# The q and k moves between partitions issued on GpSimd's DMA queue instead of SyncE's

## The chip, the cores and the metric

The kernel runs on one core of a Trainium2 chip. The metric is the device time of one launch in microseconds; shown is the median of three runs. A profiled execution of the same program gives the rows below; its own time stands beside its span.

## The reference

One transformer layer in float32 on 512 tokens and 16 meta tokens (T = 528), width 1024. `rmsnorm`, then one wide projection `u @ w_in` that yields the queries, keys and values of three kinds of attention and three gates; then a gated sum of the three, an output projection, and a gated convolutional feed-forward of width 2816.

```python
y_sb = _stick_breaking(q_sb, k_sb, v_sb)                 # 4 heads of 64
y_sp = _indexed_sparse_attention(norm(q_sp), norm(k_sp), v_sp, q_ix, k_ix, w_ix, ...)  # 4 heads, top 132 keys
y_df = _differential_attention(q1, q2, k1, k2, v_df, lam, ...)   # 4 heads, two score maps each
merged = (sigmoid(g_sb + b) * (y_sb @ w_br_sb) + sigmoid(g_sp + b) * (y_sp @ w_br_sp)
          + sigmoid(g_df + b) * (y_df @ w_br_df))
h = h + merged @ w_out
h = h + (silu(conv(gate)) * val) @ w_down                # gate, val = split(rmsnorm(h) @ w_up)
```

## The kernel before

Every float32 operand of a large product is held as two float32r parts, a high one and a rest (names ending in h and l), and a product is three passes on TensorE: high by high, rest by high, high by rest (`mm3`, L336). The third pass is the one that reads the rest of the weights, `wl`.

**Weights** come in 133 chunks of 128x1024 from `wpk`, in the order of a written plan (`PLAN`), and `prep(k)` (L315) readies them one chunk ahead of use. There are two ways. A chunk of the first kind is loaded raw by SyncE (`wr`, two buffers), cast to `wh` by ScalarE, and its rest `wl` is a subtraction on VectorE or GpSimd. Every second chunk from the eleventh to the output projection (the set `two`, L296) goes without a raw buffer: GpSimd issues a load into `wh` (`gdma`, L120), ScalarE writes minus that into `wl` (L332), and GpSimd issues a second load of the chunk that is added onto `wl` in flight (L334). In this text that is the accumulating load; there are 25. `wh` has three buffers and `wl` two, so ScalarE's write into `wl` waits until the third pass of the chunk two before it is done.

**Attention** runs in eight units: sb0, sb1, df0 to df3, sp0, sp1. For each, three dense products give raw queries, keys and values (`unit`, L1007), and between their matmuls small streams are ticked (L195) that do the rest. `q_stream` (L665) casts the queries to `a`, takes the rest `l`, and then issues three moves of 64 partitions each; `k_stream` (L683) does the same with four tiles and six moves. A move is a DMA from SBUF to SBUF which brings a head from partitions 64 to 127 to 0 to 63 or the other way, so that two heads' high and rest parts stand as one 128-row operand for `scores` (L761). In each group of three, the third move overwrites what the first two (in the keys' case) or the first (in the queries') read, and so waits until those have landed. In all 8 x 9 = 72 moves of 129 to 132 KB are issued, all by `move` (L659) on SyncE.

**Order.** The program is generated with a planner's clocks for the four engines (P TensorE, V VectorE, S ScalarE, G GpSimd). `book(e, cost)` (L77) advances one of them and the due time of the stream that is being ticked by the cost and 150 ns more. `sub` (L108) sends a subtraction to GpSimd or VectorE, whichever the clocks expect first. A unit's scores are not put into TensorE's order before the planner's clock passes the unit's due time: the time at the end of its moves plus 6500 (L681, L699) plus SLACK of 1800 (L882). A framework then sets each engine's order of instructions by its own forecast of when they become ready, and adds the semaphores. Each engine takes its instructions strictly in that order, and a DMA's waits are waited out by the engine that issues it.

**Queues.** SyncE issues the raw weights, the bias tables and, before the change, the moves. GpSimd issues the 25 + 25 loads of the second kind and the gathers of the bias tiles, and does a part of the subtractions and additions.

Of the kernel before, what the change touches and what calls it, by code (L numbers as in the profile page):

```python
# [8 lines left out]
F32 = mybir.dt.float32  # L9
# [46 lines left out]
def tile_kernel(ctx: ExitStack, tc, hT, wpk, par, bias, yT):  # L56
    nc = tc.nc
# [19 lines left out]
    def book(e, cost):  # L77
        c = cur[0]
        clock[e] = max(clock[e], clock["P"]) + cost
        c["t"] = max(clock[e], c["t"] + cost, clock["P"] + cost) + LAT  # L80
# [25 lines left out]
    G = Timed("G", nc.gpsimd, 2.3, 200)  # L106
# [550 lines left out]
        give("tmp", 4)  # L657

    def move(dst, src):  # L659
        nc.sync.dma_start(dst.bitcast(F32), src.bitcast(F32))  # L660

    def qtile():
        return ap_.tile([P, T], F32R, tag="qk", bufs=caps["qk"], name="qk")
# [1 line left out]
    def q_stream(unit, raw, gain):  # L665


        n = TQ
        if gain is not None:
            yield from headnorm(raw, n, gain, blk)  # L670
        yield from wait("qk", 2)
        yield from wait("tmp")
        a, b, l = qtile(), qtile(), tmp(F32R)
        S.copy(a[:, :n], raw[:, :n])
        sub(l[:, :n], raw[:, :n], a[:, :n])
        move(b[64:128, :n], a[64:128, :n])
        move(b[0:64, :n], l[64:128, :n])
        move(a[64:128, :n], l[0:64, :n])
        give("tmp", 2)
        unit["q"] = (a, b)  # L680
        unit["t"] = max(unit.get("t", 0), cur[0]["t"] + 6500)  # L681
# [594 lines left out]
```

## Time and profile before

| | us |
|---|---|
| three runs: median (lowest to highest) | 901.34 (894.71 to 905.32) |
| the profiled execution's own time | 900.03 |
| its span, first to last instruction | 898.2 |
| TensorE busy | 870.2 |
| VectorE busy | 536.1 |
| ScalarE busy | 454.6 |
| GpSimd busy | 248.9 |

The attention stage ends at about 470 us, the output projection at about 520, the feed-forward at 898. The moves run from 40.8 to 378.6 us. An engine's busy time does not hold its waits; idle time is given per releaser, which is inferred.

### The profile page before, as it was taken

The page shows a single profiled execution, that of the slowest core. Times are in us where ns is not written, and L with a number is a line of the kernel's source. Part 1 is how long each engine was busy: PE and PEld are TensorE (multiplying, and loading weights), DVE is VectorE, ACT ScalarE, POOL GpSimd, SP SyncE. Part 2 cuts the span into 40 slices and gives each one's busy share as a digit, 9 for nine tenths or more (in the row PEclk, how much of TensorE's full clock was granted, in tenths as well). Part 3 has the DMA queues.
Part 4 walks back from the last instruction along what each step waited for, and adds up shares of the span by engine and source line. Part 5 has one row for each costly group of instructions (what it writes and reads, how often), then busy time and mean ns, then how long its engine had stood idle before and what let it go on. Part 6 is the DMA issues. An engine that isn't in the chain of part 4 may idle for free.

```text
span 898.2 us, 15407 instructions
## 1 busy us (share of the span) xinstructions
PE 870.2 (97%) x6066; PEld 807.8 (90%) x6066; DVE 536.1 (60%) x1145; ACT 454.6 (51%) x848; POOL 248.9 (28%) x200
## 2 busy tenths in 40 slices
PE   7899999999999999799999999999999999999998
PEld 6888999999998999699999999999999999888886
DVE  7669969888887787686457544444454544322221
ACT  7457887787756687645553443333333333211110
POOL 2334012122112111664034234444444444200100
PEclk9999999999999999899999999999999999999999
DMA  6666635574547645544454323233333322333330
GB/s 235 163 177 210 163 86 124 133 168 111 121 109 156 164 105 137 120 125 92 121 118 164 96 94 94 94 94 94 95 93 95 92 88 92 103 117 106 118 104 27
DMA packets 35959, 107.79 MB, mean 120 GB/s; under 512 B 4713, under 2 KB 4857, under 8 KB 35888
## 3 DMA queue, kind: packets, MB, share of 16 engines
q1 hardware_dynamic: 27968, 78.19, 28.7%
q0 software_dynamic: 7920, 28.64, 14.9%
q8 instruction: 47, 0.77, 0.4%
q14 instruction: 24, 0.20, 0.1%
HBM read 93.99 MB, written 5.86 MB: 111 GB/s over the span
## 4 chain that ended last, share of the span: by engine, by line
PE 72%; DVE 9%; ACT 7%; DMA 6%; issue 5%; POOL 1%; SPq 1%; ACTq 0%; POOLq 0%; DVEq 0%
PE psd L183 50%; PE psw L183 21%; DVE tmp L99 4%; ACT tmp L99 3%; DMA wl<-wpk 2%; DMA qk<-qk 2%; PE psw L187 2%; DVE work L99 1%; DMA wr<-wpk 1%; DVE wl L99 1%; DMA wh<-wpk 1%; DVE m L99 1%; ACT wl L99 1%; ACT G L99 1%; ACT wh L99 1%
## 5 line engine op out<-in xcount | busy, mean ns | idle before, releaser
L99 ACT CAST wh<-wr 128x1024 fp32r<-128x1024 f32 (+2 forms) x112 | 114.1, 1021 | 201.6 <-DMA wr<-wpk 168.5
L99 DVE TENSOR_TENSOR wl<-wr,wh 128x1024 fp32r<-128x1024 f32 (+2 forms) x80 | 96.2, 1203 | 71.6 <-PE psd L183 67.9
L99 POOL TENSOR_TENSOR wl<-wr,wh 128x1024 fp32r<-128x1024 f32 x32 | 81.5, 2548 | 176.6 <-PE psd L183 95.0
L183 PE MATMUL psd<-xh,wh 128*128 128x258 f32 (+2 forms) x792 | 118.9, 289 | 4.0 <-DVE tmp L99 3.5
L183 PE MATMUL psd<-xl,wh 128*128 128x258 f32 (+2 forms) x792 | 118.2, 289 | 0.0
L183 PE MATMUL psd<-xh,wl 128*128 128x258 f32 (+2 forms) x792 | 116.7, 288 | 1.2 <-POOL wl L99 1.1
L183 PEld LDWEIGHTS psd<-xh,wh 128*128 128x128 f32 x792 | 104.7, 190 | 5.7 <-issue 3.6
L183 PEld LDWEIGHTS psd<-xh,wl 128*128 128x128 f32 x792 | 104.1, 190 | 2.4 <-POOL wl L99 1.3
L183 PEld LDWEIGHTS psd<-xl,wh 128*128 128x128 f32 x792 | 104.4, 191 | 0.5
L99 ACT ACTIVATE tmp<-tmp 128x528 f32<-128x528 f32 (+7 forms) x154 | 69.6, 475 | 17.2 <-DVE tmp L99 14.6
L99 POOL TENSOR_TENSOR ft<-ft 128x512 f32<-128x512 f32 x22 | 47.1, 2140 | 83.5 <-DVE ft L99 83.5
L99 DVE SCALAR_TENSOR_TENSOR ft<-ft,prm 128x512 f32<-128x512 f32 x44 | 48.0, 1090 | 30.1 <-ACT ft L99 29.3
L334 POOL DMA_DIRECT2D wl<-wpk x25 | 22.2, 888 | 130.1 <-ACT wl L99 105.6
L183 PE MATMUL psw<-uh,wh 128*128 128x256 f32 (+2 forms) x264 | 47.0, 320 | 0.0
L183 PE MATMUL psd<-ul,wh 128*128 128x258 f32 (+2 forms) x264 | 46.9, 319 | 0.0
L183 PE MATMUL psw<-ul,wh 128*128 128x256 f32 (+2 forms) x264 | 46.9, 319 | 0.0
L183 PE MATMUL psd<-uh,wl 128*128 128x258 f32 (+2 forms) x264 | 46.8, 319 | 0.0
L183 PE MATMUL psw<-uh,wl 128*128 128x256 f32 (+2 forms) x264 | 46.8, 319 | 0.0
L183 PE MATMUL psd<-uh,wh 128*128 128x258 f32 (+2 forms) x264 | 46.8, 319 | 0.0
L183 PE MATMUL psd<-al,wh 128*128 128x512 f32 x176 | 45.8, 396 | 0.0
L183 PE MATMUL psd<-ah,wl 128*128 128x512 f32 x176 | 45.8, 396 | 0.0
L183 PE MATMUL psd<-ah,wh 128*128 128x512 f32 x176 | 45.8, 396 | 0.0
(196 smaller groups left out, 1674.7 us busy)
## 6 DMA issues: line engine op xcount, KB each, us to landing
wr<-wpk SPq DMA_DIRECT2D x106, 512.0 KB, 3.6
wh<-wpk POOLq DMA_DIRECT2D x25, 512.0 KB, 3.9
wl<-wpk POOLq DMA_DIRECT2D x25, 512.0 KB, 5.6
qk<-qk SPq DMA_DIRECT2D x48, 132.0 KB, 2.5
gd<-tab SPq DMA_DIRECT2D x8, 328.0 KB, 5.5
tmp<-hT SPq DMA_DIRECT2D x8, 264.0 KB, 6.2
W<-gd POOLq DMA_DIRECT2D x8, 264.0 KB, 3.9
qk<-tmp SPq DMA_DIRECT2D x16, 128.5 KB, 4.4
```

The lines of the kernel that those rows point to most:

```text
L99: return f(out, *a, **k)
L183: PE.matmul(out, lhsT, rhs, **k)
L187: PE.transpose(out, x, ident[:x.shape[0], :x.shape[0]])
L334: nc.gpsimd.dma_start(wl, chunk(a), accum_op=OP.add)
```

## The change

`move` issues its DMA on GpSimd's queue, and books 650 ns on the planner's GpSimd clock, which also puts 650 + 150 ns on the stream's due time for each move. Nothing else is edited; sources, destinations and the dependences among the moves are as before.

```diff
     def move(dst, src):
-        nc.sync.dma_start(dst.bitcast(F32), src.bitcast(F32))
+        book("G", 650)
+        nc.gpsimd.dma_start(dst.bitcast(F32), src.bitcast(F32))
```

## Rows read from the trace of the kernel before

**Rows 1.** The page: span, then each engine's busy time and share

```profile
span 898.2 us, 15407 instructions
PE 870.2 (97%) x6066; PEld 807.8 (90%) x6066; DVE 536.1 (60%) x1145; ACT 454.6 (51%) x848; POOL 248.9 (28%) x200
```

**Rows 2.** Waits of TensorE and GpSimd: total us, times, longest us

```profile
PE psw L183 <- DMA qk<-qk: 2.5, 2, 1.9
...
POOL wl L334 <- ACT wl L99: 105.6, 18, 12.9
```

**Rows 3.** Waits of SyncE's queue, same columns

```profile
SPq L312 <- DVE wl L99: 454.3, 70, 18.2
SPq L312 <- POOL wl L99: 171.5, 30, 9.2
...
SPq L660 <- DMA qk<-qk: 24.5, 21, 3.2
```

**Rows 4.** The page's DMA issues: count, size, median us from issue to landing

```profile
wr<-wpk SPq DMA_DIRECT2D x106, 512.0 KB, 3.6
wh<-wpk POOLq DMA_DIRECT2D x25, 512.0 KB, 3.9
```

**Rows 5.** The moves' line: ns min/median/max of an issue; landing times

```profile
L660 SPq DMA_DIRECT2D qk<-qk x56: 461/471/1907, 40.8 to 378.6; - x56
...
DMA to landing us min/median/max: 2.2/2.8/7.2
```

**Rows 6.** Groups by line on POOL and DVE: busy us, mean ns, idle before

```profile
L122 POOL DMA_DIRECT2D wh<-wpk x25 | 14.3, 570 | 55.6 <-PE psd L183 45.5 <-PE psw L183 6.2 <-PE psw L187 3.8
...
L99 DVE TENSOR_TENSOR wl<-wr,wh 128x1024 fp32r<-128x1024 f32 (+2 forms) x80 | 96.2, 1203 | 71.6 <-PE psd L183 67.9 <-ACT wh L99 3.6
```

**Rows 7.** Timeline of GpSimd in sb1, df0, df3: start us, us, what [idle before]

```profile
79.91 1.35 POOL L99 TENSOR_TENSOR qk<-tmp,qk 128x528 fp32r<-128x528 f32 x1 [0.88 <-ACT qk L99]
84.85 0.93 POOL L334 DMA_DIRECT2D wl<-wpk  x1 [3.59 <-ACT tmp L99]
...
157.83 1.87 POOL L99 TENSOR_TENSOR qk<-tmp,qk 128x528 fp32r<-128x528 f32 x1 [6.01 <-ACT qk L99]
163.15 0.89 POOL L334 DMA_DIRECT2D wl<-wpk  x1 [3.45 <-ACT wl L99]
...
296.27 1.34 POOL L99 TENSOR_TENSOR qk<-tmp,qk 128x528 fp32r<-128x528 f32 x1 [5.52 <-ACT qk L99]
299.11 0.90 POOL L334 DMA_DIRECT2D wl<-wpk  x1 [1.50 <-ACT wl L99]
```

**Rows 8.** Landing of the accumulating loads issued at 84.85, 163.15, 299.11

```profile
DMA to landing us min/median/max: 9.1/9.1/9.1
...
DMA to landing us min/median/max: 5.4/5.4/5.4
...
DMA to landing us min/median/max: 7.5/7.5/7.5
```

**Rows 9.** Timeline of TensorE: the first third-pass matmuls that read those three

```profile
93.96 1.23 PE L183 MATMUL psd<-xh,wl 128*128 128x258 f32 x8
...
169.26 1.13 PE L183 MATMUL psd<-xh,wl 128*128 128x258 f32 x8
...
307.74 1.11 PE L183 MATMUL psd<-xh,wl 128*128 128x258 f32 x8
```

**Rows 10.** Timeline of SyncE's queue: the six key moves of df0

```profile
157.77 5.29 SPq L660 DMA_DIRECT2D qk<-qk  x6
```

**Rows 11.** Timeline of TensorE: scores that waited for moves (df2, sp0)

```profile
281.38 0.48 PE L183 MATMUL psw<-qk 128*2 128x16 f32 x3 [1.93 <-DMA qk<-qk]
...
368.97 0.34 PE L183 MATMUL psw<-qk 128*2 128x16 f32 x2 [3.62 <-issue]
```

**Rows 12.** Windows: stretch, length, busy us of PE, PEld, DVE, ACT, POOL; clock

```profile
280.00:284.00 4.00, 2.62 (x15) 2.56 (x16) 1.23 (x8) 2.46 (x7) 2.11 (x2) 0.71 0.84 225
...
370.00:374.00 4.00, 3.77 (x19) 3.40 (x19) 3.91 (x15) 2.50 (x8) 2.25 (x2) 0.55 0.07 15
```

## The prediction, made before the changed kernel was run

> **What bounds the kernel now.** I read the page first. TensorE is busy 870.2 of 898.2 us [rows 1], so the kernel lasts as long as TensorE's order of matmuls plus its holes, 28 us in all, and a change on other engines counts only where it makes or closes a hole. GpSimd is busy 28% [rows 1]; as a sum of work it has room for any number of moves. But each engine takes its instructions in order, so the question is not GpSimd's load: it is what stands behind a move while the move waits.
>
> Next, the waits. TensorE itself waited for moves 2.5 us by name [rows 2]; in the timeline one such hole is 1.93 us at 281.38, and a hole of 3.62 us at 368.97, put down to "issue", stands before the same kind of matmul, sp0's first scores [rows 11]. So the moves are exposed in two units and hidden in six. SyncE's queue waited 454.3 + 171.5 us for raw weight buffers to be freed [rows 3]: its loads start when a buffer is free, and a queue without moves brings almost none of them sooner. I count no gain there.
>
> The last view is the timeline of GpSimd beside TensorE's, and it carries the forecast. The accumulating load of a second-kind chunk can only be issued late, and TensorE wants it soon after it lands. In sb1 it is issued at 84.85 [rows 7], lands 9.1 us later, at 93.95 [rows 8], and TensorE starts the third pass that reads it at 93.96 [rows 9]: no slack at all. In df0 163.15 + 5.4 = 168.55 against 169.26, 0.7 us of slack. In df3 299.11 + 7.5 = 306.61 against 307.74, 1.1 us. What delays these issues on GpSimd by more than the slack is a hole in TensorE. And the key moves fall just there: the subtraction that precedes them ends 3.6, 3.5 and 1.5 us before the accumulating load.
>
> **The change part by part.** *Removed:* 72 issues on SyncE of 471 ns [rows 5] and the 21 waits there, 24.5 us, for the moves that a third move must follow [rows 3]. SyncE is waiting for buffers anyway: 0 us.
>
> *Added to GpSimd:* 72 issues. The trace has no SBUF-to-SBUF move on that queue. The nearest row is the load of `wh`, 570 ns each [rows 6]; from below the price is SyncE's 471 ns. I take 570: 41 us of GpSimd's time in a stretch of 338 us, which costs nothing by itself. Landing: from issue to landing a 512 KB load takes 3.6 us on SyncE and 3.9 on GpSimd [rows 4], so I add 0.3 us to each landing that a third move waits for.
>
> *A group of six key moves on GpSimd.* On SyncE df0's six took 5.29 us with both waits [rows 10]. On GpSimd: 5.29 + 6 x 0.1 + 2 x 0.3 = 6.5 us, in which GpSimd does nothing else, after the subtraction that it has just done. If all six stand ahead of the accumulating load, that load comes late by:
> - sb1: 79.91 + 1.35 + 6.5 = 87.8, against 84.85: 2.9 us, slack 0, hole 2.9.
> - df0: 157.83 + 1.87 + 6.5 = 166.2, against 163.15: 3.05 us, slack 0.7, hole 2.3.
> - df3: 296.27 + 1.34 + 6.5 = 304.1, against 299.11: 5.0 us, slack 1.1, hole 3.9.
> - df1 shows the same pattern (keys subtracted just before an accumulating load); I give it the mean of df0 and df3, 3.1.
> In the other units no accumulating load with little slack follows the key moves closely. Together 12.2 us. From below it is 0: the framework orders GpSimd by its own forecast, and may put the accumulating load ahead of the moves, or between the fourth and those that wait. Nothing in the trace tells where. I take half, 6.1 us.
>
> *The clock.* The hole at 281.38 was followed by a granted clock of 0.71 over 280 to 284, the one at 368.97 by 0.55 over 370 to 374 [rows 12]; 0.29 x 4 = 1.2 and 0.45 x 4 = 1.8 us of work lost, 1.5 on average. Holes of 2 to 4 us are what the four units would give; I count two of the four, 3.0 us, with bounds of 0 and 6.0.
>
> *The two exposed units.* Their moves come later by the subtraction that GpSimd must finish before it issues the first (1.34 to 1.87 us) and by 6.5 - 5.29 = 1.2, together 2.7 us. Against that the booking shifts the due time: six moves of 800 ns put the scores 4.8 us further back in TensorE's order, so other matmuls come first. Bounds: both holes and their clock gone, -(1.93 + 3.62 + 3.0) = -8.6; both longer by 2.7, +5.4. I take 0.
>
> Sum: 6.1 + 3.0 + 0 = +9.1 us on the profiled execution's 900.03, whose span is 898.2. That gives 909.1; the median of the runs shown lies 1.3 higher, so 910 on it, +1.0%.
>
> **A rule of the skill against the row.** GpSimd's plain DMA issues took 570 ns on average [rows 6] while VectorE was busy 60% of the span [rows 1], and landed only 0.3 us behind SyncE's: I see no blocking by VectorE in them. The Trainium skill, "SBUF — State Buffer", section "SBUF: two separate sides", warns that GpSimd cannot write a DMA's descriptors while VectorE holds the port they share, which would speak against this change. By the rows nothing is added for it; by that rule each move could wait for one VectorE instruction, and the case is a rival below.
>
> **The rivals.**
> - *Hidden.* The accumulating loads go first, or the holes are filled. For it: three of four GpSimd microseconds are idle, and five units have their scores long after their moves. Against it: slacks of 0 to 1.1 us. The time: 0 to +3 us, 900 to 904. The Trainium skill, "DMA: Bandwidth & Descriptors", section "Issuing engines are not separate DMA queues", gives this outcome: another issuing engine only saves the sequencer's time.
> - *Moves held behind GpSimd's own waits.* GpSimd waits 105.6 us in all, up to 12.9 at once, for ScalarE before an accumulating load [rows 2]; moves queued behind it are late by that. The cover is the planned 6.5 + 1.8 us and the 4.8 of the booking in the units whose scores come straight after their keys (sb0, df2, sp0). Unlike the likeliest case the delay is in the scores, and it decides from a wait of some 8 us on. Price: 12.9 - 8.3 = 4.6 us in each of three units, 14 on top of the 9: about 924.
> - *VectorE blocks the issues.* Each of six moves held by one VectorE subtraction of 1203 ns [rows 6] makes a group 7.2 us longer; in four units 29 us, about 939. Against it stands the 570 ns.
> - *Faster.* The planner's 4.8 us takes the scores of df2 and sp0 out of the place where they wait for moves: -8.6 us with the clock, if at the same time the accumulating loads go ahead of the moves. It decides that both happen; 893 at best, about 890 if some of the VectorE work held up behind sp0's scores comes earlier too.
> - That the edit does nothing of what it says is excluded: 72 issues change queue, one can count them.
>
> **How the numbers follow.** The likeliest case, late accumulating loads, has 0.50 and its own range of 904 to 916; hidden 0.20 (896 to 904); moves held 0.17 (916 to 930); VectorE 0.03; faster 0.10 (885 to 896). 1% of 901.34, about what a measurement of this kernel can tell from no change, is 9 us: slower means over 910.4, faster under 892.3. The likeliest case straddles the upper bound, half on each side. Slower: 0.25 + 0.17 + 0.03 = 0.45. Same: 0.25 + 0.20 and a fifth of faster, 0.47. Faster: 0.08. The range leaves out most of faster, the VectorE case and the far end of moves held, 2 in 10 together: 897 to 926.
>
> **What would show it.** In the changed profile: 72 issues at L661 on POOL of about 570 ns; GpSimd's timeline with moves between the key subtraction and the accumulating load in sb1, df0, df1, df3; landings of those loads after TensorE wanted them, as waits of TensorE for DMA `wl` of 2 to 4 us that are not there now; granted clock under 1 after them. Waits of moves for `qk` landings of some 2.5 us as GpSimd's idle time. It is wrong if the accumulating loads keep their times, if the holes at 281 and 369 close, or if the extra time sits in the feed-forward, which has no moves.

## The result and the profile after

The changed kernel took 910.5 us, the median of four runs (906.74 to 915.87), beside 898.21 of the kernel before on the same chip (894.71 to 905.32): a ratio of 1.0146, 95% interval 1.010 to 1.019. It is slower by about 13 us. The profiled execution's span is 904.6 us against 898.2.

The page of the changed kernel, answering to [rows 1]:

```profile
span 904.6 us, 15393 instructions
PE 870.5 (96%) x6066; PEld 805.6 (89%) x6066; DVE 546.5 (60%) x1148; ACT 450.3 (50%) x848; POOL 280.9 (31%) x269
```

TensorE is busy for the same time as before; what was added is holes.

The page's list of waits of TensorE in the changed kernel (total us, times, longest), answering to [rows 2]:

```profile
PE psw L183 <- DVE mx L99: 7.4, 4, 5.5
PE psw L183 <- ACT tmp L99: 5.5, 3, 3.1
PE psw L183 <- ACT wh L99: 5.1, 1, 5.1
PE psd L183 <- DMA wl<-wpk: 4.0, 4, 1.3
```

The same list in the kernel before:

```profile
PE psw L183 <- ACT wh L99: 5.3, 1, 5.3
...
PE psw L183 <- ACT tmp L99: 1.8, 2, 1.5
...
PE psd L183 <- DMA wl<-wpk: 0.7, 1, 0.7
```

The wait for VectorE at the head of the list is new, the second one, for ScalarE's `tmp`, has grown from 1.8 us, and the third was there before; the wait for moves by name is gone. Where the new ones are shows best by stages. Each of the chunks counted here ends with a third pass on TensorE, 16 matmuls that read `wl`, so counting these in the timeline marks the progress of the dense work (the matmuls that do not belong to attention). The stages below, worked out from those ends, are: to the end of the 6th chunk, to the 12th, to the 45th, the 46th chunk alone (the first of the second branch, the product of df's output with its weights, which wants the outputs of all four df units), to the 60th (the first of the output projection), and the rest.

| us | to 6th | to 12th | to 45th | 46th | to 60th | rest | span |
|---|---|---|---|---|---|---|---|
| before | 52.1 | 53.0 | 254.9 | 20.5 | 100.5 | 417.1 | 898.2 |
| changed | 47.9 | 52.8 | 248.2 | 36.9 | 101.7 | 417.1 | 904.6 |

The first stage ends between 47 and 54 us in all kernels here, whatever the edit (see the end), and so is left out of comparisons. Of what is left, the stretch up to the 45th chunk is 6.7 us shorter and the 46th chunk 16.4 us longer. The two windows of that chunk, before and changed (start and end, length, busy us of PE, PEld, DVE, ACT, POOL with counts, granted clock, DMA share, GB/s):

```profile
360.10:380.60 20.50, 15.00 (x86) 12.86 (x86) 13.14 (x45) 12.84 (x35) 12.31 (x13) 0.83 0.57 126
```

```profile
348.90:385.80 36.90, 23.64 (x134) 19.01 (x133) 25.13 (x73) 19.81 (x56) 19.78 (x27) 0.72 0.26 56
```

In both, apart from the chunk itself, TensorE has only attention work there, in scraps. Before, the window holds 5.5 us of idle time and 86 matmuls at a mean granted clock of 0.83. In the changed kernel it lasts 36.9 us, 13.3 us of it idle, with 134 matmuls at a mean clock of 0.72, a mixture of the two levels. Priced as the prediction priced the clock, missing share times length, this is 10.3 us against 3.5 before (an estimate), so the added idle time, 7.8 us, and the added loss by the clock, 6.8, weigh about the same.

What TensorE idles for in it can be followed back through three engines in the changed kernel. TensorE's timeline (start us, us, what, [idle before]):

```profile
358.50 1.23 PE L183 MATMUL psw<-tmp,ones 128*128 128x258 f32 x2 [3.08 <-ACT tmp L99]
...
366.37 1.22 PE L183 MATMUL psw<-tmp,ones 128*128 128x256 f32 x2 [5.52 <-DVE mx L99]
...
378.56 0.87 PE L183 MATMUL psd<-y,wh 128*128 128x258 f32 x5 [0.50 <-ACT y L99]
```

VectorE's:

```profile
365.86 0.44 DVE L99 CUSTOM_DVE_ANT_0 tmp<-psw,tmp 128x272 f32<-128x272 f32 x1 [4.42 <-POOL tmp L99]
...
368.46 0.31 DVE L99 CUSTOM_DVE_ANT_0 tmp<-psw,tmp 128x144 f32<-128x144 f32 x1 [0.91 <-POOL tmp L99]
...
376.62 0.73 DVE L99 SCALAR_TENSOR_TENSOR tmp<-tmp,gsub 128x514 f32<-128x514 f32 x1
```

GpSimd's:

```profile
357.99 1.27 POOL L99 TENSOR_TENSOR tmp<-tmp,qk 128x514 fp32r<-128x514 f32 x1 [6.28 <-ACT qk L99]
359.21 0.56 POOL L661 DMA_DIRECT2D qk<-qk  x1
359.76 0.55 POOL L661 DMA_DIRECT2D qk<-tmp  x1
361.00 1.02 POOL L661 DMA_DIRECT2D qk<-qk  x2 [0.69 <-ACT qk L99]
363.00 0.52 POOL L661 DMA_DIRECT2D qk<-tmp  x1 [0.98 <-DMA qk<-qk]
363.51 1.54 POOL L661 DMA_DIRECT2D qk<-qk  x3
365.05 0.78 POOL L99 TENSOR_TENSOR tmp<-W,work 128x272 f32<-128x272 f32 x1
```

The last line is the addition of a bias tile for sp0's softmax (in `weights_sp`). It stands behind eight of sp1's nine moves. VectorE needs it and waits 4.42 us; behind it in VectorE's order stands the norm of df3's output (the line with `gsub` at 376.62), and the second branch's matmuls that read that output start at 378.56.

The places the prediction named look otherwise. GpSimd's timeline in sb1, df0, df1 and df3, answering to [rows 7]:

```profile
77.86 1.35 POOL L99 TENSOR_TENSOR qk<-tmp,qk 128x528 fp32r<-128x528 f32 x1 [6.87 <-ACT qk L99]
79.17 1.06 POOL L661 DMA_DIRECT2D qk<-qk  x2
80.22 0.97 POOL L334 DMA_DIRECT2D wl<-wpk  x1
...
152.51 1.32 POOL L99 TENSOR_TENSOR qk<-tmp,qk 128x528 fp32r<-128x528 f32 x1 [6.59 <-ACT qk L99]
153.79 2.07 POOL L661 DMA_DIRECT2D qk<-qk  x4
155.85 0.98 POOL L334 DMA_DIRECT2D wl<-wpk  x1
157.21 0.56 POOL L661 DMA_DIRECT2D qk<-qk  x1 [0.38 <-issue]
158.50 0.53 POOL L661 DMA_DIRECT2D qk<-qk  x1 [0.72 <-DMA qk<-qk]
...
182.96 1.58 POOL L661 DMA_DIRECT2D qk<-qk  x3
184.52 0.98 POOL L334 DMA_DIRECT2D wl<-wpk  x1
...
286.82 0.97 POOL L334 DMA_DIRECT2D wl<-wpk  x1
...
295.83 2.07 POOL L661 DMA_DIRECT2D qk<-qk  x4
300.53 1.05 POOL L661 DMA_DIRECT2D qk<-qk  x2 [2.63 <-DMA qk<-qk]
301.58 0.96 POOL L334 DMA_DIRECT2D wl<-wpk  x1
```

The framework set the accumulating load after two moves in sb1, four in df0 and three in df1, ahead of those that wait. Only in df3 do all six stand before a load, and it is not the load that the prediction priced: counted from the start, the one at 299.11 before is the 15th accumulating load, which here goes at 286.82, ahead of the key moves, since the dense work runs earlier. The one at 301.58 is the 16th. It landed 6.7 us later, at 308.28, and TensorE read it at that moment, after a gap of 0.14 us:

```profile
308.28 0.64 PE L183 MATMUL psd<-xh,wl 128*128 128x264 f32 x3
```

The moves' line itself (ns min/median/max of an issue, then landing), answering to [rows 5]:

```profile
L661 POOL DMA_DIRECT2D qk<-qk x56: 516/526/997, 38.0 to 367.4; - x56
...
DMA to landing us min/median/max: 2.2/3.1/6.8
```

### The profile page after: what moved, and what is told of

The parts are those of the page before. It is cut to its first block, busy times and chain, and to the rows that moved or that the text cites. A ratio compares the mean times of both kernels' runs of the same rounds, so it can differ in the third digit from the quotient of the medians.

```text
span 904.6 us, 15393 instructions
## 1 busy us (share of the span) xinstructions
PE 870.5 (96%) x6066; PEld 805.6 (89%) x6066; DVE 546.5 (60%) x1148; ACT 450.3 (50%) x848; POOL 280.9 (31%) x269
## 4 chain that ended last, share of the span: by engine, by line
PE 52%; issue 3%; DMA 3%; DVE 2%; POOL 2%; ACT 1%; POOLq 0%; ACTq 0%
PE psd L183 34%; PE psw L183 18%; DMA wl<-wpk 2%; DVE tmp L99 1%; ACT tmp L99 1%; POOL tmp L99 1%; DMA qk<-qk 1%; POOL G L99 1%; PE psw L187 1%; DVE ml L99 0%; DVE wl L99 0%; DVE pmw L99 0%; POOL y L99 0%; DVE G L99 0%; POOL wh L122 0%
## 5 line engine op out<-in xcount | busy, mean ns | idle before, releaser
L99 DVE TENSOR_TENSOR wl<-wr,wh 128x1024 fp32r<-128x1024 f32 (+2 forms) x80 | 99.1, 1240 | 70.8 <-PE psd L183 59.1
L99 POOL TENSOR_TENSOR wl<-wr,wh 128x1024 fp32r<-128x1024 f32 x32 | 78.3, 2450 | 156.5 <-ACT wh L99 64.6
L183 PE MATMUL psd<-xh,wh 128*128 128x258 f32 (+2 forms) x792 | 117.0, 287 | 2.1 <-DVE tmp L99 1.2
L99 DVE SCALAR_TENSOR_TENSOR ft<-ft,prm 128x512 f32<-128x512 f32 x44 | 50.2, 1141 | 26.7 <-ACT ft L99 25.9
L183 PE MATMUL psd<-ul,wh 128*128 128x258 f32 (+2 forms) x264 | 46.9, 319 | 0.0
L183 PE MATMUL psd<-uh,wl 128*128 128x258 f32 (+2 forms) x264 | 46.9, 319 | 0.0
```

Source lines behind the costliest of these rows:

```text
L99: return f(out, *a, **k)
L183: PE.matmul(out, lhsT, rhs, **k)
```

## The experiments

The edit has two parts, a queue and a booking, and the moves belong to units that stand differently. The prediction blamed accumulating loads behind moves; the profile after suggests two others: the booking, which puts scores later in TensorE's order, and the bias additions behind sp1's moves. All ratios are to the kernel before, on the same chip, with 95% intervals; the profiles' stages stand in the table at the end of this section.

### The booking alone

```diff
     def move(dst, src):
+        book("G", 650)
         nc.sync.dma_start(dst.bitcast(F32), src.bitcast(F32))
```

> The moves stay on SyncE, each still books 650 ns on the planner's GpSimd clock: TensorE's order is that of the changed kernel but for a few lines. Order theory (the booking alone costs the time: scores 4.8 us later in TensorE's order, the second branch then waits for df3): about 908 to 911 beside 898 to 901 of the kernel before, with a TensorE hole of some 10 us between 350 and 380 us. Queue theory (GpSimd's additions for sp0's scores stand behind moves on its queue): 896 to 902, VectorE's wait of 4.4 us for GpSimd at 366 us gone. Prediction's theory (accumulating loads late behind moves): 898 to 902.

Measured: 908.7 us, 1.0108 (1.007 to 1.0147). No DMA changed its queue, and it costs some 10 us. The 46th chunk takes 32.6 us. GpSimd's bias additions are not in the way here (VectorE waits for one of them 1.22 us, at 378.75); the order itself costs. The window of the 46th chunk, columns as above:

```profile
352.40:385.00 32.60, 26.18 (x134) 21.44 (x133) 25.91 (x74) 19.52 (x56) 15.55 (x18) 0.69 0.29 63
```

Idle time is 6.4 us against 5.5 before: what has grown is the attention work that is left for this chunk, at a lower clock.

This is not all of it: TensorE waited 5.04 us at 84.12 in sb1, which neither the kernel before nor the changed one does. TensorE's timeline of this kernel:

```profile
84.12 0.21 PE L183 MATMUL psw<-ident,pmw 128*16 128x2 f32 x2 [5.04 <-ACT pmw L99]
```

ScalarE, which TensorE waits for, waited for raw weights, and their load stood on SyncE behind two of sb1's moves. ScalarE's and SyncE's timelines of this kernel, then SyncE's in the changed one:

```profile
81.97 1.04 ACT L99 CAST wh<-wr 128x1024 fp32r<-128x1024 f32 x1 [7.09 <-DMA wr<-wpk]
...
73.62 1.12 SPq L661 DMA_DIRECT2D qk<-tmp  x2
74.83 0.87 SPq L312 DMA_DIRECT2D wr<-wpk  x1
...
64.55 0.33 SPq L312 DMA_DIRECT2D wr<-wpk  x1
```

With the moves on GpSimd the load goes 10 us earlier. The hole is in all three profiled kernels that book and leave sb1's moves on SyncE (4.4 to 5.0 us), and in none that books and has them on GpSimd.

### The queue alone

```diff
     def move(dst, src):
-        nc.sync.dma_start(dst.bitcast(F32), src.bitcast(F32))
+        nc.gpsimd.dma_start(dst.bitcast(F32), src.bitcast(F32))
```

> The moves go to GpSimd, nothing is booked: TensorE's order is that of the kernel before but for a few lines. Order theory: as before, 898 to 902. Queue theory: slower by 3 to 10 us, with a hole near 365 us that ends on GpSimd's additions or on late moves of sp0 (the old hole of 3.6 us longer). Prediction's theory: about 906 to 910, the loss as waits of TensorE for DMA wl of 1 to 4 us each in sb1, df0, df1, df3.

Measured: 912.55 us, 1.015 (1.0108 to 1.0193). As dear as both parts together, so the two prices don't add up. TensorE's timeline of this kernel, at the first scores of df2, df3 and sp0, answering to [rows 11]:

```profile
277.96 0.17 PE L183 MATMUL psw<-qk 128*2 128x16 f32 x1 [2.02 <-DMA qk<-qk]
...
308.97 0.45 PE L183 MATMUL psw<-qk 128*2 128x16 f32 x3 [2.86 <-DMA qk<-qk]
...
370.98 0.34 PE L183 MATMUL psw<-qk 128*2 128x16 f32 x2 [3.86 <-issue]
...
374.29 1.04 PE L183 MATMUL psw<-qk 128*2 128x16 f32 x4 [2.98 <-POOL tmp L99]
```

Two of these waits were there before (1.93 and 3.62), two are new. None is a wait for `wl` in sb1, df0, df1 or df3; TensorE's waits for `wl` come to 1.9 us, all after 400 us.

### Which units: sp's moves back on SyncE, and only sp's on GpSimd

```diff
-    def move(dst, src):
+    def move(dst, src, unit):
         book("G", 650)
-        nc.gpsimd.dma_start(dst.bitcast(F32), src.bitcast(F32))
+        q = nc.gpsimd if unit["kind"] != "sp" else nc.sync
+        q.dma_start(dst.bitcast(F32), src.bitcast(F32))
```

Left out here are the lines that hand the unit to `move`.

> The changed kernel with the booking for all, but the 18 moves of sp0 and sp1 on SyncE; the 54 of sb and df stay on GpSimd. Queue theory: most of the loss gone, 898 to 903, no wait of VectorE for GpSimd's additions near 366 us. Order theory: 908 to 911 as the changed kernel. Prediction's theory: about 908, since the four places it names (sb1, df0, df1, df3) are unchanged.

Measured: 903.55 us, 1.0062 (1.0029 to 1.0095). Moving 18 of the 72 back takes away more than half of the loss. The 46th chunk falls from 36.9 to 32.0 us.

The complement (`== "sp"`), with the booking for all:

> The booking for all, the 18 moves of sp0 and sp1 on GpSimd, the 54 of sb and df on SyncE. Queue theory: nearly the whole loss, 906 to 911, with VectorE's wait of some 4 us for GpSimd near 366 us. Order theory: 908 to 911. Prediction's theory: 898 to 902.

Measured: 912.31 us, 1.0145 (1.0102 to 1.0188), the 46th chunk 39.5 us. By the pair, sp's moves on GpSimd are what the queue costs under the booking: 36.9 - 32.0 = 4.9 and 39.5 - 32.6 = 6.9 us in that one chunk. The 54 others cost nothing there. On GpSimd they spare the kernel the hole in sb1: the stage to the 12th chunk takes 57.5 to 57.9 us in the three kernels that book with them on SyncE, and 52.8 to 54.4 in the three that book with them on GpSimd. So some 3 to 5 us of what the booking costs alone are not in the changed kernel.

### The due time alone

```diff
     def move(dst, src):
+        cur[0]["t"] += 800
         nc.sync.dma_start(dst.bitcast(F32), src.bitcast(F32))
```

> All moves on SyncE; instead of the booking each move adds 800 ns to the due time of its stream, and the planner's GpSimd clock is left alone. If the later due times of the scores make the stretch without dense work around 350 to 385 us: 906 to 911, as with the booking (908.7). If it is the GpSimd clock, which sends subtractions elsewhere: 899 to 902.

Measured: 908.78 us, 1.0095 (1.0061 to 1.0129), the same as the booking on SyncE. So it is the later due time of the scores, and the planner's GpSimd clock is not needed for it.

### The bias additions on VectorE, in the changed kernel

```diff
-            G.tensor_tensor(b[:, :n], wt[:, 384 - P * i:384 - P * i + n], negs[i], OP.add)
+            book("G", G.cost(b[:, :n]))
+            nc.vector.tensor_tensor(b[:, :n], wt[:, 384 - P * i:384 - P * i + n], negs[i], OP.add)
```

> The changed kernel, all moves on GpSimd and booked, but the 20 additions of the bias for the sparse scores run on VectorE (the planner still books them on GpSimd, so that its order stays). If those additions standing behind sp1's moves on GpSimd cost the 5 us by which sp's moves on GpSimd are dearer than on SyncE: 904 to 907 with no wait of VectorE for GpSimd near 366 us. If VectorE's own work there is the bound: 909 to 913.

Measured: 903.04 us, 1.0057 (1.002 to 1.0093): with all 72 moves on GpSimd, some 8 us less than the changed kernel by the ratios, though VectorE has more to do. The 46th chunk is at 31.8 us, as with sp's moves on SyncE, and VectorE no longer waits for GpSimd in it. This is the chain read above, confirmed by its removal.

The same edit in the two orders without the booking:

> The kernel before, moves on SyncE and nothing booked for them, with the 20 additions of the bias for the sparse scores on VectorE instead of GpSimd (still booked on GpSimd). If these additions on GpSimd cost time only because moves stand in front of them: 898 to 901, as the kernel before. If they are late in the kernel before too: 894 to 897, a version faster than both.

Measured: 896.85 us, 0.9994 (0.9967 to 1.0022). Without moves in front of them the additions cost nothing on GpSimd; no version faster than both came out of it.

> All moves on GpSimd, nothing booked, and the 20 additions on VectorE. With them on GpSimd this order took 912.6. If what it loses to the kernel before is the additions standing behind moves (a wait of 3.0 us at 374): 904 to 908. If it is the moves that land later for scores which follow at once (waits of 2.0, 2.9 and 3.9 us at 278, 309 and 371): 909 to 912.

Measured: 911.82 us, 1.0154 (1.0114 to 1.0195): no gain. In the order without booking it is the moves' landing, and not the additions, that the scores wait for; the wait of 2.98 us at 374 came back as one of 3.00 us for moves.

### Only the early units on GpSimd

Nothing booked; first the 18 moves of sb0 and sb1 alone on GpSimd, then those of sb0, sb1, df0 and df1.

```diff
     def move(dst, src, unit):
-        nc.sync.dma_start(dst.bitcast(F32), src.bitcast(F32))
+        q = nc.gpsimd if unit["kind"] in ("sb0", "sb1", "df0", "df1") else nc.sync
+        q.dma_start(dst.bitcast(F32), src.bitcast(F32))
```

> No booking, so TensorE's order is that of the kernel before; only the 18 moves of sb0 and sb1 go to GpSimd, the other 54 stay on SyncE. By the theory of three parts (the early moves gain some 3 to 5 us on GpSimd because SyncE's queue is full of bias tables there; the late ones of df2, df3 and sp lose; the booking loses): 894 to 898 beside 900, the second chunk run by 100 us ahead of the kernel before by 3 to 4 us and the rest unchanged. If the early gain is only time given back later: 899 to 901.

Measured: 899.82 us, 1.0013 (0.9978 to 1.0048). The early gain that I expected from comparing single profiles did not come; what I had compared lay within the scatter of the first 50 us (see the end).

> Nothing booked; the moves of sb0, sb1, df0 and df1 on GpSimd, those of df2, df3, sp0 and sp1 on SyncE. If the loss of the queue alone (912.6 with all 72 on GpSimd) sits in the last four units, whose scores follow their moves closely or meet a crowded GpSimd: 897 to 901, as the kernel before, with no new waits of TensorE. If accumulating loads behind the moves of sb1, df0 and df1 cost, as the prediction had it: 902 to 907, with waits for DMA wl of 1 to 3 us there.

Measured: 898.94 us, 1.0018 (0.9987 to 1.0048). 36 moves change queue for nothing, among them those of sb1, df0 and df1, three of the four places that the prediction priced. So, without a booking, the loss of the queue sits in the last four units.

### The accumulating loads made later

Three small additions on GpSimd, whose results are not used, between ScalarE's write of `wl` and the load:

```diff
             S.activation(wl, wh, AF.Copy, scale=-1.0)
+            pad = wp.tile([P, P], F32, tag="pad", bufs=1, name="pad")
+            for j in range(3):
+                nc.gpsimd.tensor_tensor(pad, wl[:, j], wh[:, j], OP.add)
             book("G", 1050)
```

> The kernel before with three small additions on GpSimd (some 1.4 us together, not booked) between ScalarE's write of wl and each of the 25 accumulating loads; their results are not used. If the slack of those loads is what the prediction read (0.04 to 5 us, 10 of the 25 under 1.4): the sum of what exceeds the slack, some 7 us: 905 to 909, as waits of TensorE for DMA wl of about 1 us each. If the loads have more room than they seem: 900 to 902.

Measured: 910.65 us, 1.0136 (1.0082 to 1.019). TensorE's waits in this kernel (total, times, longest):

```profile
PE psd L183 <- DMA wl<-wpk: 11.0, 9, 2.7
```

Before it was 0.7 us, once. The three additions take 1.4 us; so small a delay at every load costs as much as the whole change did, and in sum the slack is as small as it was read. Place by place the reading holds less well: of the four loads that the prediction priced only df0's made TensorE wait (0.92 us at 172.41); sb1's, read as having none, landed 1.1 us sooner after its issue than before (7.98 us instead of 9.07). And the change does not delay the loads in this way.

### The due time earlier

```diff
-        unit["t"] = max(unit.get("t", 0), cur[0]["t"] + 6500)
+        unit["t"] = max(unit.get("t", 0), cur[0]["t"] + 4100)
```

The same line is changed twice, in `q_stream` and in `k_stream`.

> The kernel before with the constant in the due time of a unit's scores lowered from 6500 to 4100. The due times cost in one direction (4.8 us later: 908.8). If earlier is better: 895 to 898, the stretch from 360 to 380 shorter. If the present value stands between two losses, the scores then wait for moves more often (the holes of 1.9 and 3.6 us grow): 901 to 906.

Measured: 903.18 us, 1.006 (1.0032 to 1.0087). TensorE's waits for moves by name rise from 2.5 to 6.4 us (281.75, 283.82 and 378.50, in df2 and sp0). 2.4 us earlier loses 5 us, 4.8 us later loses 8.5: the due time before stands between two losses.

The stages of all profiles, in us:

| | to 12th | to 45th | 46th | to 60th | sum | timed ratio |
|---|---|---|---|---|---|---|
| before | 53.0 | 254.9 | 20.5 | 100.5 | 428.9 | 1 |
| changed | 52.8 | 248.2 | 36.9 | 101.7 | 439.6 | 1.0146 |
| booking alone | 57.5 | 247.1 | 32.6 | 101.1 | 438.3 | 1.0108 |
| due time alone | 57.9 | 247.9 | 35.5 | 95.9 | 437.2 | 1.0095 |
| queue alone | 53.9 | 260.2 | 23.9 | 104.9 | 442.9 | 1.0150 |
| sp on SyncE | 54.4 | 248.5 | 32.0 | 100.8 | 435.7 | 1.0062 |
| only sp on GpSimd | 57.9 | 248.1 | 39.5 | 99.2 | 444.7 | 1.0145 |
| additions on VectorE | 54.3 | 249.0 | 31.8 | 100.8 | 435.9 | 1.0057 |
| first four on GpSimd | 53.0 | 252.6 | 19.3 | 102.5 | 427.4 | 1.0018 |
| late loads | 53.4 | 256.7 | 20.7 | 105.7 | 436.5 | 1.0136 |
| sb on GpSimd | 54.5 | 255.1 | 19.5 | 102.4 | 431.5 | 1.0013 |
| before, additions on VectorE | 53.3 | 253.5 | 20.3 | 100.7 | 427.8 | 0.9994 |
| queue alone, additions on VectorE | 54.0 | 260.2 | 24.0 | 103.2 | 441.4 | 1.0154 |
| due time earlier | 53.1 | 259.6 | 20.9 | 100.4 | 433.9 | 1.0060 |

The sums follow the timed ratios within some 5 us. With the later due time (six rows) the scores go later, dense work runs 6 to 8 us ahead up to the 45th chunk, and the 46th costs 11 to 19 us more, because the branch waits for attention that has been put off. Without it, the queue's price is spread: 5.3 us in the stage up to the 45th chunk, 3.4 in the 46th and 4.4 after it.

## Why the prediction was right or wrong, point by point

The time came out where it was forecast, 910.5 for 910, and that is luck: it came about by another way than its sum said. Of the sum's two terms neither is in the trace where it was put. Two of the prediction's own signs of being wrong came: the holes at 281 and 369 closed, and in sb1, df0 and df1 the accumulating loads went ahead of the moves that wait and cost TensorE no wait.

- **What bounds the kernel** held: TensorE's work is unchanged and holes decide; GpSimd's 28% of busy time was no protection. A SyncE queue without moves, priced at nothing, brought nothing as long as nothing was booked (first four units: 1.0018); under the booking it spares the hole in sb1, 3 to 5 us.
- **The prices of a move** held. 526 ns an issue against the 570 taken, a median landing 0.3 us later (3.1 against 2.8) as taken; that median mixes sizes, and for the 48 moves of 132 KB, all of them keys' moves, it went from 2.5 to 3.5. df3's six moves took 295.83 to 301.58, 5.75 us against 6.5.
- **The accumulating loads, 6.1 us, and the clock behind them, 3.0 us:** this step failed. TensorE's waits for `wl` rose from 0.7 to 4.0 us, and the trace has none at the four places; they are at 344, 451, 463 and 475 us. That the loads have little slack was read rightly in sum, as the late loads show (11.0 us of waits); wrong was the half that I gave to "the moves stand ahead of it". In sb1, df0 and df1 the framework placed the load ahead of the moves that wait, as the bound of 0 said. In df3 the priced load had gone before the key moves, at 286.82; the next one, behind all six, cost a gap of 0.14 us. I had laid the new moves over the old times of the loads, but the change shifts both.
- **The two exposed units, 0 with bounds of -8.6 and +5.4:** this step failed too. I counted the booking's 4.8 us only as relief for scores that wait for moves. Those waits did go, but the due time alone costs 8.5 us and the booking alone 9.7, both past the upper bound. Of this 3 to 5 us are the hole in sb1, which the changed kernel does not have; what the later order costs in the changed kernel itself is 5 to 6 us, by the two runs that keep the booking and take the other loss away (1.0062 and 1.0057). I had not asked what else is due next. The second branch wants df3's output; scores put off by 4.8 us in each unit that follows its keys closely put that off too, and the dense work that could have filled the gap had been done earlier.
- **What stands behind a move:** the right question with the wrong victim. I looked for GpSimd instructions with little slack in the timeline and found the loads; the bias additions of sp0, which VectorE waits for, are in the same timeline and I did not price them. With sp's moves on SyncE or the additions on VectorE 7 to 8 us of the 13 go.
- **The clock** was the right kind of price, at another place and larger: 0.72 over 36.9 us in the 46th chunk, against 0.83 over 20.5 before; 10.3 against 3.5 us by the prediction's own reckoning (an estimate), where it took 3.0 behind single holes [rows 12].
- **The rivals.** *Hidden* is what the first four units do. *Moves held behind GpSimd's waits*: GpSimd waited 27.2 us in 15 times for landings of moves, but in none of the six kernels with the later due time does TensorE wait for a move by name; with the queue alone, where nothing puts the scores off, it does (2.02 and 2.86 us, and 3.86 put down to "issue"). *VectorE blocks the issues*: half of the issues took 526 ns or less and none over 997. The Trainium skill, "SBUF — State Buffer", section "SBUF: two separate sides", says that GpSimd cannot write a DMA's descriptors while VectorE holds the port they share; these issues show little sign of it, and no run here isolated it. *Faster* fell: both of its conditions were met in part, the waits of df2 and sp0 went and the loads mostly kept ahead of the moves that wait, and the kernel was still slower.

The prices don't add (1.0108 and 1.015 give 1.0146 together), because each part repairs a hole of the other: the queue the one in sb1, the booking those at df2's, df3's and sp0's scores. What is left in the changed kernel is 5 to 6 us for the later order and 7 to 8 for the additions behind sp's moves, an estimate from ratios that are each known to some 0.4%. What stays open is the queue alone: its new waits named above come to about 6 us of its 13.5, and the 4.4 us after the 46th chunk were not followed to a cause.

## What to carry to other kernels

Before moving a DMA to a queue of an engine that computes, list every instruction behind it on that engine and follow each to its consumer, the urgent-looking ones and the plain ones alike; an engine that is idle 70% of the time still holds up what stands behind a wait. A cost booked in a planner is a change of order of its own: measure the booking and the queue apart, since either alone may carry the loss, and look for the holes that one part closes for the other. When two traces are laid side by side, number the repeated instructions: what stands at the same place may be the next one of its kind. And where a deferred piece of work has a consumer further on, ask what fills the engine when that consumer comes: running ahead with the filler early is no gain.

## What the runs showed that I had not expected

The first 50 us scatter by themselves: the 6th chunk ended between 46.9 and 54.2 us in profiles of kernels whose edits hardly touch that stretch (52.1 in the kernel before, 46.9 with only the bias additions moved, which come after 350 us). TensorE's timeline of the changed kernel, ahead of its first move at 38.0 us:

```profile
28.28 0.95 PE L183 MATMUL psd<-xh,wh 128*128 128x258 f32 x6 [0.53 <-DVE tmp L99]
```

The same matmul in the kernel with sb0's and sb1's moves alone on GpSimd:

```profile
32.03 0.77 PE L183 MATMUL psd<-xh,wh 128*128 128x258 f32 x2 [5.50 <-DVE tmp L99]
```

A window of that kernel around it (columns as in the windows above):

```profile
28.00:36.00 8.00, 3.96 (x18) 4.00 (x19) 6.34 (x14) 4.65 (x11) 1.12 (x1) 0.57 0.36 112
```

A wait of 0.53 or of 5.50 us, and after the long one a granted clock of 0.57: together 5.0 us and, by the same reckoning as above, 0.43 x 8 = 3.4 us, an estimate of 8.4 us beside a spread of the kernel's runs of 10.6 (894.71 to 905.32), and more than half of what the change costs. That this wait makes the spread of the timed runs is not shown. A single profile compared by absolute times would have credited it to the edit, as I did before the run with sb's moves alone.
